# One order of accumulator banks for all four weight units of a transposed feed-forward chunk

## The chip, the cores and the metric

The kernel runs on one core of one Trainium2 chip. The metric is the device time of one execution in microseconds (us). Three runs are compared by their median, and one more execution was taken with a profile.

## What is computed

A two-layer decoder trunk over 256 tokens of width 1024, in float32. Each layer has four post-norm blocks: a SwiGLU feed-forward half-step, an attention mixer (forgetting attention in layer 0, latent attention in layer 1), a second feed-forward half-step, and a gated per-layer input embedding. The part that matters here is the half-step, which is run four times:

```python
D_MODEL, SEQ, DEPTH, D_FF = 1024, 256, 2, 2816
ALPHA = (2 * DEPTH) ** 0.25

def swiglu(x, w_in, w_out):
    h = x @ w_in
    gate, up = h[..., :D_FF], h[..., D_FF:]
    return (jax.nn.silu(gate) * up) @ w_out

def post_norm(x, delta, g, b):
    return layer_norm(ALPHA * x + delta, g, b)

for i in range(DEPTH):
    x = post_norm(x, 0.5 * swiglu(x, ffn1_w_in[i], ffn1_w_out[i]), ...)
    x = post_norm(x, mix(x), ...)
    x = post_norm(x, 0.5 * swiglu(x, ffn2_w_in[i], ffn2_w_out[i]), ...)
    x = post_norm(x, gate * (p[i] @ ple_w_proj[i]), ...)
```

## The kernel before

Every product of float32 matrices is made of three matmuls on split operands: both factors are written as a high part and a low remainder in a reduced format, and `mm3` adds high x high, high x low and low x high into one accumulator. ScalarE makes the high part of a weight unit (line 171) and VectorE the remainder (line 172). Such a split fills one of a handful of slots (`hl0` to `hl9`, and `qk`, `fs`, `ota`, `otb` when they are lent).

The order of the work is written out by hand. Weights come in groups over the DMA queue of SyncE into three raw buffers, and a planner (`Stream`) decides where in the instruction stream the next unit is split: `pump`, called at the end of each `mm3`, compares a running estimate of each engine's time with the arrival of the next group. That estimate grows by the number of columns of each matmul. `use` hands out a unit, and splits it first if it isn't split yet.

A feed-forward half-step (`ffn`) works through 11 chunks of 256 hidden columns, each with its gate and its up half. Chunks 0 and 1 are made token-major (`H`, in the first half-step partly by `first`): for each half of the tokens (`t`) the gate and the up half land side by side in one accumulator bank. Then `act` reads the bank, ScalarE with Silu over the gate half (line 630) and VectorE with a multiply by the up half (line 631). `T` transposes chunk 0 with four transposes.

Chunks 2 to 10 are unit-major and transposed (`HT`), in three groups: 2, 3, 4, then 5, 6, 7, then 8, 9, 10, with the output products (`W`) of finished chunks after each group, and four transposes ahead of the second group and of the third. An HT chunk takes two banks, `ps[0]` for the gate and `ps[1]` for the up half; the ring of banks is `h` for even chunks and `tr` for odd ones, with two banks each. `H` takes one bank of `h` at a time. Of its four weight units (`u`), each holds two slices of the contraction (`kk`), and each slice has four blocks of 128 hidden columns (`b`): blocks 0 and 1 go to `ps[0]`, blocks 2 and 3 to `ps[1]`. One block of one slice is one `mm3`, that is three weight loads and three matmuls of 256 columns, so a unit has 24 matmuls and a chunk 96. When all four units are through, ScalarE applies Silu to `ps[0]` (line 663), VectorE multiplies by `ps[1]` (line 664), and the product is split in two parts (lines 496 and 497) as the stationary operand of `W`.

A first write into a bank waits until the last reader of the tile that stood there is done; the wait stands at the first weight load of that write. All matmuls of `mm` have line 487, all transposes line 491.

Of the kernel before, what the change touches and what calls it, by code (L numbers as in the profile page):

```python
# [394 lines left out]
class Trunk:  # L395
# [180 lines left out]
    def ffn(self, li, which, lni, kv=False, ple=False, at=None, cold=False):  # L576
# [69 lines left out]
        def HT(c):  # L646
            ring = "h" if c % 2 == 0 else "tr"
            ps = [self.bank(ring) for _ in range(2)]
            for u in range(4):
                w = self.use(("win", li, which, c, u))  # L650
                steps = [(kk, b) for kk in range(2) for b in range(4)]
                if u == 0:
                    steps.sort(key=lambda s: s[1] // 2)
                for kk, b in steps:
                    k = 2 * u + kk
                    o = ps[b // 2][:, 256 * (b % 2) : 256 * (b % 2) + 256]
                    col = slice(512 * kk + 128 * b, 512 * kk + 128 * b + 128)
                    self.mm3(
                        o, lambda i: w[:, i, col], lambda i: self.xT[:, :, i, k, :],
                        k == 0 and b % 2 == 0, k == 7 and b % 2 == 1,  # L660
                    )
            gt = self.tl([128, 768], F32, "P", 2)[:, 0:512]
            nc.scalar.activation(gt, ps[0], AF.Silu)  # L663
            nc.vector.tensor_tensor(gt, gt, ps[1], op=ALU.mult)  # L664
            self.S.busy(act=512, dve=512)
            o = self.tl([128, 2, 512], F32R, "g4", 5)
            self.parts(o[:, 0, :], o[:, 1, :], gt)
            gT[c] = o
# [31 lines left out]
        for i, group in enumerate(GROUPS):  # L700
            if i == 1:
                T(1, "h")
            if i == 2:
                if kv:
                    self.kv_transpose()
                elif ple:
                    self.ple_transpose()
                else:
                    spare = self.bank("tr")
                    for k in range(4):  # L710
                        self.transpose(spare[:, 128 * k : 128 * k + 128], self.ident)
            for c in group:
                for f in at.get(c, ()):
                    f()
                if c == 4:
                    self.load_gb(li, lni)
                HT(c)
            if i == 1 and kv:
                self.flush()
                self.kv_transpose_rope()  # L720
            if i == 2 and ple:
                self.ple_project(li)
            while late and (late[0] <= group[-1]) and not (i == 0 and late[0] == 1):
                W(late.pop(0), both)
# [780 lines left out]
```

## Time and profile before

| | |
|---|---|
| three runs | 1097.37, 1095.62, 1091.08 us |
| median | 1095.62 us |
| profiled execution | 1097.88 us, span 1095.7 us |
| mean granted TensorE clock | 0.997 |
| TensorE matmuls busy | 1078.4 us, 7160 matmuls |
| VectorE busy | 711.9 us |
| ScalarE busy | 540.7 us |
| HBM read | 196.81 MB, 181 GB/s over the span with what is written |

Rows of the timeline and of the chain of waits begin with the start in microseconds from the begin of the span and the length in microseconds; then come the engine, the line, and the tiles written and read ("h<-xT,hl": bank of ring h, from the activations and a weight slot), and how many instructions are merged in the row. PE is TensorE's matmul, PEld its weight load, DVE VectorE, ACT ScalarE, POOL GpSimd and SP SyncE. Matmuls overlap in the pipeline, so the pace of a row is read from the distance of two starts. The view of one line ends with those who waited for it. A group row ends with the busy time in microseconds, the mean of one in nanoseconds, and the idle time before with its releaser.

### The profile page before, as it was taken

What the parts mean: (1) busy time and instruction counts of PE and PEld (TensorE: products, weight loads), DVE (VectorE), ACT (ScalarE), POOL (GpSimd) and SP (SyncE); (2) the same over time, 40 slices, a digit from 0 to 9 for tenths busy, and PEclk for the clock granted to TensorE, in tenths of its full rate; (3) what the DMA queues carried; (4) which work ended last, traced back from release to release, by engine and by line L of the source; (5) the groups of instructions that cost most, each with busy time, mean ns of one, the idle gap of its engine ahead of it and who ended that gap; (6) DMA issues with size and microseconds to landing.
All of it is one profiled execution on the core that took longest, in us unless ns stands there. A gap on an engine that the chain in (4) does not pass through costs nothing.

```text
span 1095.7 us, 17634 instructions
## 1 busy us (share of the span) xinstructions
PE 1078.4 (98%) x7160; PEld 978.4 (89%) x7160; DVE 711.9 (65%) x1010; ACT 540.7 (49%) x792; POOL 76.5 (7%) x128
## 2 busy tenths in 40 slices
PE   9999999999999999999999999999999999999997
PEld 6999999899879999998899999988999789898986
DVE  5665545788797545558966554388666885555566
ACT  5564433666646444444565443345655464444431
POOL 0000000222200000000320000011111000000000
PEclk9999999999999999999999999999999999999999
DMA  8886652444358856455578554344453668565502
GB/s 274 289 283 236 195 187 93 154 151 158 118 162 280 286 166 192 153 187 161 162 278 265 191 177 166 93 104 132 142 163 103 194 220 290 194 203 192 174 19 77
DMA packets 150676, 199.00 MB, mean 182 GB/s; under 512 B 11842, under 2 KB 128578, under 8 KB 150596
## 3 DMA queue, kind: packets, MB, share of 16 engines
q1 hardware_dynamic: 150596, 197.88, 55.7%
q8 instruction: 56, 0.92, 0.3%
q14 instruction: 24, 0.20, 0.1%
HBM read 196.81 MB, written 1.05 MB: 181 GB/s over the span
## 4 chain that ended last, share of the span: by engine, by line
PE 88%; DVE 7%; ACT 2%; issue 1%; POOL 1%; DMA 0%; DVEq 0%; SPq 0%; ACTq 0%; POOLq 0%
PE h L487 36%; PE y L487 30%; PE tr L487 19%; DVE hl L172 2%; PE tr L491 2%; DVE x L564 1%; DVE st L549 1%; DVE x L548 1%; ACT hl L171 1%; POOL rs L559 1%; PE y L465 1%; DMA raw<-in_ffn_w_in_dram 0%; DVE xT L497 0%; PE tr L1021 0%; DVE g L790 0%
## 5 line engine op out<-in xcount | busy, mean ns | idle before, releaser
L172 DVE TENSOR_TENSOR hl<-raw,hl 128x1024 fp32r<-128x1024 f32 (+3 forms) x287 | 333.6, 1183 | 159.7 <-ACT hl L171 158.5
L171 ACT ACTIVATE hl<-raw 128x1024 fp32r<-128x1024 f32 (+3 forms) x287 | 285.3, 1018 | 185.0 <-PE y L487 87.3
L487 PE MATMUL h<-xT,hl 128*128 128x256 f32 x2064 | 245.1, 279 | 0.9 <-DVE qk L497 0.9
L487 PEld LDWEIGHTS h<-xT,hl 128*128 128x128 f32 x2064 | 240.5, 188 | 2.1 <-DVE qk L497 1.1
L487 PE MATMUL y<-hl,g 128*128 128x512 f32 x780 | 181.0, 390 | 0.0
L487 PEld LDWEIGHTS y<-hl,g 128*128 128x128 f32 x780 | 145.7, 188 | 29.8
L487 PE MATMUL tr<-xT,hl 128*128 128x256 f32 x888 | 105.5, 278 | 0.0
L487 PEld LDWEIGHTS tr<-xT,hl 128*128 128x128 f32 x888 | 103.6, 188 | 0.1
L487 PE MATMUL h<-hl,xT 128*128 128x512 f32 (+1 forms) x396 | 94.5, 388 | 0.7 <-DVE xT L497 0.4
L487 PEld LDWEIGHTS h<-hl,xT 128*128 128x128 f32 x396 | 72.4, 188 | 17.1 <-DVE xT L497 1.1
L487 PE MATMUL y<-hl,xT 128*128 128x512 f32 (+2 forms) x312 | 60.8, 349 | 0.2 <-DVE xT L497 0.2
L487 PEld LDWEIGHTS y<-hl,xT 128*128 128x128 f32 x312 | 50.7, 188 | 7.5 <-DVE xT L497 0.7
L559 POOL TENSOR_TENSOR rs<-ve,mhalf 128x1 f32<-128x1 f32 x16 | 15.2, 950 | 525.0 <-DVE ve L558 525.0
L496 ACT ACTIVATE xT<-tr 128x512 fp32r<-128x512 f32 x34 | 19.2, 597 | 57.9 <-PE tr L491 57.9
L497 DVE TENSOR_TENSOR g<-P,g 128x512 fp32r<-128x512 f32 x36 | 24.9, 692 | 25.2 <-ACT g L496 25.2
L496 ACT ACTIVATE g<-P 128x512 fp32r<-128x512 f32 x36 | 22.8, 632 | 31.0 <-DVE P L664 31.0
L487 PE MATMUL y<-hl,ota 128*128 128x512 f32 x144 | 36.9, 400 | 0.0
L172 DVE TENSOR_TENSOR qk<-raw,qk 128x1024 fp32r<-128x1024 f32 x21 | 25.7, 1223 | 10.7 <-ACT qk L171 10.5
L172 DVE TENSOR_TENSOR otb<-raw,otb 128x1024 fp32r<-128x1024 f32 (+1 forms) x20 | 24.0, 1202 | 13.1 <-ACT otb L171 13.1
L663 ACT ACTIVATE P<-h 128x512 f32<-128x512 f32 x20 | 12.0, 598 | 41.5 <-PE h L487 41.5
L664 DVE TENSOR_TENSOR P<-P,h 128x512 f32<-128x512 f32 x20 | 13.7, 687 | 27.8 <-PE h L487 26.1
L487 PEld LDWEIGHTS y<-hl,ota 128*128 128x128 f32 x144 | 26.8, 193 | 5.2
(240 smaller groups left out, 1399.3 us busy)
## 6 DMA issues: line engine op xcount, KB each, us to landing
raw<-in_ffn_w_in_dram SPq DMA_DIRECT2D x172, 512.0 KB, 5.1
raw<-in_ffn_w_out_dram SPq DMA_DIRECT2D x44, 1024.0 KB, 5.2
raw<-in_fox_w_in_dram SPq DMA_DIRECT2D x12, 1024.0 KB, 5.3
raw<-in_ple_w_gate_dram SPq DMA_DIRECT2D x8, 1024.0 KB, 5.0
raw<-in_mla_w_o_dram SPq DMA_DIRECT2D x8, 1024.0 KB, 5.0
gb<-in_ln_g_dram SPq DMA_DIRECT2D x8, 512.0 KB, 7.0
gb<-in_ln_b_dram SPq DMA_DIRECT2D x8, 512.0 KB, 7.5
raw<-in_fox_w_o_dram SPq DMA_DIRECT2D x4, 1024.0 KB, 5.1
```

Source lines behind the costliest of these rows:

```text
L171: nc.scalar.activation(hi[:, c], src[:, c], AF.Copy)
L172: nc.vector.tensor_tensor(lo[:, c], src[:, c], hi[:, c].bitcast(F32), op=ALU.subtract)
L465: self.nc.tensor.matmul(hot[:, 0:384], self.mask[:, 0:128], self.mask, start=True, stop=True)
L487: self.nc.tensor.matmul(out, lhsT, rhs, start=start, stop=stop)
L491: self.nc.tensor.transpose(out, in_, self.ident)
L496: self.nc.scalar.activation(hi, src, AF.Copy)
L497: self.nc.vector.tensor_tensor(lo, src, hi.bitcast(F32), op=ALU.subtract)
L548: nc.vector.scalar_tensor_tensor(xs, xs, alpha, y, op0=ALU.mult, op1=ALU.add)
L549: nc.vector.bn_stats(st, xs)
L559: nc.gpsimd.tensor_tensor(rs, ve, self.mhalf, op=ALU.pow)
L663: nc.scalar.activation(gt, ps[0], AF.Silu)
L664: nc.vector.tensor_tensor(gt, gt, ps[1], op=ALU.mult)
```

## The change

In unit 0 of every HT chunk the eight steps (slice, block) stood sorted by bank: slice 0 blocks 0, 1, slice 1 blocks 0, 1, and then slice 0 blocks 2, 3, slice 1 blocks 2, 3. Now they stand as in the other three units: slice 0 blocks 0, 1, 2, 3 and then slice 1 blocks 0, 1, 2, 3. The set of matmuls, their operands and the start and stop flags of each bank stay as they are.

```diff
             for u in range(4):
                 w = self.use(("win", li, which, c, u))
-                steps = [(kk, b) for kk in range(2) for b in range(4)]
-                if u == 0:
-                    steps.sort(key=lambda s: s[1] // 2)
-                for kk, b in steps:
+                for kk, b in ((kk, b) for kk in range(2) for b in range(4)):
                     k = 2 * u + kk
                     o = ps[b // 2][:, 256 * (b % 2) : 256 * (b % 2) + 256]
                     col = slice(512 * kk + 128 * b, 512 * kk + 128 * b + 128)
```

## The prediction

> **What bounds the kernel now.** I read the page first: the busy shares, the granted clock and the chain that ended last.
>
> ```profile
> span 1095.7 us, 17634 instructions
> ...
> PE 1078.4 (98%) x7160; PEld 978.4 (89%) x7160; DVE 711.9 (65%) x1010; ACT 540.7 (49%) x792; POOL 76.5 (7%) x128
> ...
> PEclk9999999999999999999999999999999999999999
> ...
> PE 88%; DVE 7%; ACT 2%; issue 1%; POOL 1%; DMA 0%; DVEq 0%; SPq 0%; ACTq 0%; POOLq 0%
> ```
>
> TensorE is busy for 98% of the span at an undiminished clock, and 88% of the chain is its own work. Whatever holds a matmul of a transposed chunk (HT) back is therefore paid in full, and whatever doesn't costs nothing. The chain in order of time then gives the pace of the chunks. There are 36 HT chunks in twelve groups of three (three groups to a feed-forward half-step), and here is one row of 96 matmuls from each group.
>
> ```profile
> 32.59 11.31 PE h L487 x96
> ...
> 88.75 10.90 PE tr L487 x96
> ...
> 143.62 10.90 PE h L487 x96
> ...
> 336.56 11.31 PE h L487 x96
> ...
> 392.70 11.31 PE tr L487 x96
> ...
> 448.87 10.90 PE h L487 x96
> ...
> 560.39 10.90 PE h L487 x96
> ...
> 615.26 10.90 PE tr L487 x96
> ...
> 670.38 11.31 PE h L487 x96
> ...
> 897.15 11.31 PE h L487 x96
> ...
> 953.32 10.90 PE tr L487 x96
> ...
> 1008.19 10.90 PE h L487 x96
> ```
>
> The reader is to see that the same instructions run at two paces: 11.31 / 96 = 117.8 ns a matmul in five groups, 10.90 / 96 = 113.5 ns in seven. Nothing in the code separates the five from the seven: the middle group is slow in one half-step and fast in three, with the same instructions around it. A slow chunk costs 0.41 us more, a slow group about 1.23 us. All five together, 6.2 us, are nearly the spread of the three runs shown (1091.08 to 1097.37), so I take the pace for something that each execution draws anew. The profiled execution took 1097.88 us, 2.26 above the median of 1095.62; two slow groups more than the median run would account for that.
>
> Third, the timeline of single units asks whether the order inside a unit has a price of its own. Each chunk has four weight units of 24 matmuls; unit 0 alone has the sorted order today.
>
> ```profile
> 43.73 2.99 PE L487 MATMUL tr<-xT,qk 128*128 128x256 f32 x24
> 46.56 2.99 PE L487 MATMUL tr<-xT,fs 128*128 128x256 f32 x24
> 49.39 5.82 PE L487 MATMUL tr<-xT,hl 128*128 128x256 f32 x48
> ...
> 110.37 5.60 PE L487 MATMUL tr<-xT,hl 128*128 128x256 f32 x48
> 115.81 2.88 PE L487 MATMUL tr<-xT,ota 128*128 128x256 f32 x24
> 118.53 2.88 PE L487 MATMUL tr<-xT,otb 128*128 128x256 f32 x24
> ```
>
> Read the distances between starts. In the slow chunk unit 0 (sorted, slot qk) takes 46.56 - 43.73 = 2.83 us and unit 1 (alternating, slot fs) takes 49.39 - 46.56 = 2.83 us. In the fast chunk units 0 and 1 together take 115.81 - 110.37 = 5.44, that is 2 x 2.72, and unit 2 takes 118.53 - 115.81 = 2.72. Sorted and alternating cost the same to 0.01 us in either pace.
>
> **The change, part by part.** *Order of matmuls.* In unit 0 of each of the 36 chunks two triples of block columns 2 and 3 (second bank, first contraction slice) change places with two of columns 0 and 1 (first bank, second slice): 12 matmuls with their 12 weight loads are moved, none added or taken away. By the unit rows the price is 36 x 0.00 = 0; bounded by the 0.01 us that those rows resolve, at most 36 x 0.01 = 0.36 us either way.
>
> *What is not moved.* The planner is called after each triple and counts only columns, which are equal, so each split of a weight unit and each DMA that it triggers is issued behind the same number of triples; SP's and POOL's queues are passed by nothing. The unit is split as a whole before its first matmul, and both slices of the activations were already used by the chunks before, so no operand is wanted before it is there. Unit 3 is unchanged, so the activation and the multiply behind the chunk start as they did.
>
> *The wait that comes forward.* The first write to the second bank stands at matmul 13 today and at matmul 7 afterwards. It has to wait until the bank's last reader is through. From the second chunk of each group on, and in the groups that begin with chunks 5 and 8, that reader is the multiply of line 664 of the same ring's previous chunk, or a set of transposes, at least a whole chunk earlier (10.9 us or more); its cover stays huge. Only chunk 2, the first of each half-step, follows at once on an H chunk that used the same bank: its reader is the multiply of line 631. The view of that line:
>
> ```profile
> L631 DVE TENSOR_TENSOR g<-g,h x8: 406/420/422, 27.1 to 897.2; 128x256 f32<-128x256 f32 x8
> ...
> who waited for it (us, times):
> busy tenths in 40 slices 0000000000000000000000000000000000000000
> ```
>
> Nobody waits for it today. The four places where chunk 2 begins, each as the first seven weight loads and the multiply that they run against:
>
> ```profile
> 32.32 0.89 PEld L487 LDWEIGHTS h<-xT,hl 128*128 128x128 f32 x7
> ...
> 32.60 0.42 DVE L631 TENSOR_TENSOR g<-g,h 128x256 f32<-128x256 f32 x1 [1.05 <-ACT g L630]
> ...
> 336.29 0.89 PEld L487 LDWEIGHTS h<-xT,hl 128*128 128x128 f32 x7
> ...
> 336.57 0.42 DVE L631 TENSOR_TENSOR g<-g,h 128x256 f32<-128x256 f32 x1 [1.26 <-ACT g L630]
> ...
> 560.12 0.89 PEld L487 LDWEIGHTS h<-xT,hl 128*128 128x128 f32 x7
> ...
> 560.41 0.42 DVE L631 TENSOR_TENSOR g<-g,h 128x256 f32<-128x256 f32 x1 [1.05 <-ACT g L630]
> ...
> 896.88 0.89 PEld L487 LDWEIGHTS h<-xT,hl 128*128 128x128 f32 x7
> ...
> 897.17 0.42 DVE L631 TENSOR_TENSOR g<-g,h 128x256 f32<-128x256 f32 x1 [0.67 <-ACT g L630]
> ```
>
> A load of this group takes 0.19 us (the row of its group is the first of the next fence), so in the first place the seventh begins at 32.32 + 0.89 - 0.19 = 33.02; the multiply ends at 32.60 + 0.42 = 33.02. In the others it is 336.99 against 336.99, 560.82 against 560.83, 897.58 against 897.59. The seventh load would start just as its release comes, so what counts is how long a release travels from VectorE to a weight load:
>
> ```profile
> L487 PEld LDWEIGHTS h<-xT,hl 128*128 128x128 f32 x2064 | 240.5, 188 | 2.1 <-DVE qk L497 1.1
> ...
> 225.00 0.42 DVE L497 TENSOR_TENSOR qk<-h,qk 128x256 fp32r<-128x256 f32 x1
> ...
> 225.48 0.30 PEld L487 LDWEIGHTS h<-xT,hl 128*128 128x128 f32 x2 [1.08 <-DVE qk L497]
> ```
>
> 225.48 - 225.42 = 0.06 us. So each of the four is held for about 0.06 us: 4 x 0.06 = 0.24 us. Queued behind the held load on TensorE are all the rest of chunk 2, and through it everything later; other engines have slack. Today the release has six matmuls more, 6 x 0.118 = 0.70 us, of cover. The price lies between 0 (a load that hides inside the matmul before it) and 4 x 0.70 = 2.8 us, all of the cover used up, where the multiply is late; I take 0.24, since all four places lie within 0.01 us of the same alignment.
>
> *The pace.* A held load lets the matmul stream of chunk 2's group start again, and the rows show that a group keeps the pace with which it started. So four groups draw again: three that were slow here (32, 336, 896) and one that was fast (560). Bounds: all four fast, 3 x 1.23 = 3.7 us won; all four slow, 1.23 lost, on this execution. No row shows a hold this short in the middle of such a group, so I take the shares of the twelve rows, five slow to seven fast, before as after, which adds nothing to a median.
>
> *A rule that speaks against it.* By the page's clock row the granted clock stands at nine tenths or more in all 40 slices, though units 1 to 3 go through both banks twice each. The Trainium skill, "TensorE: Matmul & The Clock Gate", section "A second HAM failure mode: psum-queue depth-cycling", warns that cycling through the banks makes small idles that throttle the clock; if it held here, unit 0 would run slow too, while the trace's alternating units disagree with it.
>
> **Sum.** On the profiled execution with its paces kept, 1097.88 + 0.24 = 1098.1 us; on the median run 1095.62 + 0.24 = 1095.9 us, which is my forecast: no change that can be told. About 0.5% (5.5 us) is what a measurement of this kernel tells from no change; its three runs lie 6.3 us apart.
>
> **The rivals.**
> 1. *The multiply is late, and the wait is a real one: slower.* VectorE also carries the splits in order; one of 1.2 us ahead of line 631 would end the multiply that much later. The bracket of 0.67 to 1.26 us idle before the four multiplies speaks against it; only an idle that falls to nothing would begin to cost. From then on each place costs what the multiply is late, at most 0.70 us: 1095.62 + 2.8 = 1098.4. Chance 0.12.
> 2. *The held load leaves its group at the fast pace: faster.* For it: seven of twelve groups are fast. Against: three of the four chunk 2 groups started slow. On the profiled execution 1097.88 + 0.24 - 3.7 = 1094.4. Chance 0.12.
> 3. *It leaves its group at the slow pace: slower.* 1097.88 + 0.24 + 1.23 = 1099.4; from a run in which all four are fast it would be 4 x 1.23 + 0.24 = 5.2 us. Chance 0.09.
> 4. *Alternation halves the clock in unit 0.* 36 units of 2.72 us would take twice that, 98 us more: 1194. The equal units 0 and 1 above speak against it. Chance 0.01. This is what the skill's rule on bank cycling would come to.
>
> **How the numbers follow.** The forecast keeps 0.66. Within it the draw of the paces may put one median beyond 0.5%, 0.08 on either side (0.053 each). Of rival 1 I give a quarter to slower than that (0.03), of rival 2 three tenths to faster (0.036), of rival 3 four tenths to slower (0.036), and rival 4 wholly (0.01): faster 0.09, slower 0.13, the same 0.78. The range: at the low end the profiled execution without its five slow groups, 1097.88 - 6.2 + 0.24 = 1091.9, and the fastest run shown, 1091.08, so 1091.0; at the high end the profiled execution with rival 1's full price, 1097.88 + 2.8 = 1100.7. Rival 4 and the tails are left out.
>
> **What would show it.** Right: a waits view with a few hundredths of a microsecond of weight loads for line 631, four times, at the seventh load of chunk 2; unit 0 as long as unit 1 in every chunk; groups in only the two paces, with their number of slow ones telling the total to about 1.2 us each. Rival 1 would show line 631 among the releasers with several tenths, and VectorE busy up to the multiply. Rivals 2 and 3 would show all four chunk 2 groups at one pace, in more than one run. Wrong altogether: a change in the pace of groups that begin with chunk 5 or 8 in all runs alike, a third pace, unit 0 longer or shorter than unit 1, or other counts of splits and DMAs between the matmuls.

## The result and the profile after

| | kernel before | changed kernel |
|---|---|---|
| median of 20 runs, us | 1095.72 | 1096.30 |
| lowest to highest, us | 1091.08 to 1099.90 | 1093.70 to 1099.73 |
| profiled execution, us (span) | 1097.88 (1095.7) | 1096.81 (1094.7) |

The ratio after to before is 1.0003, with a 95% interval of 0.9992 to 1.0015: no change that can be told. The page of the changed kernel has the same instructions and shares:

```profile
span 1094.7 us, 17634 instructions
...
PE 1077.1 (98%) x7160; PEld 976.9 (89%) x7160; DVE 713.1 (65%) x1010; ACT 541.1 (49%) x792; POOL 76.5 (7%) x128
...
PEclk9999999999999999999999999999999999999999
...
PE 87%; DVE 7%; ACT 2%; issue 1%; DMA 1%; POOL 1%; SPq 0%; DVEq 0%; ACTq 0%; POOLq 0%
```

The chain in order of time, with the row of the first chunk of each of the twelve groups (start, length, engine, tile and line, matmuls):

```profile
32.08 11.36 PE h L487 x96
...
88.25 10.90 PE tr L487 x96
...
143.12 10.90 PE h L487 x96
...
335.96 10.98 PE h L487 x96
...
390.92 10.90 PE tr L487 x96
...
445.79 10.90 PE h L487 x96
...
557.30 11.36 PE h L487 x96
...
613.52 10.90 PE tr L487 x96
...
668.63 11.31 PE h L487 x96
...
897.32 10.98 PE h L487 x96
...
952.28 10.90 PE tr L487 x96
...
1007.15 10.90 PE h L487 x96
```

Two things are to be seen. The first chunk of a group took 11.31 or 10.90 us before; the four that are chunk 2 now take 11.36, 10.98, 11.36 and 10.98, that is 0.05, 0.08, 0.05 and 0.08 more, 0.26 us in all. These are the four holds, and no other chunk has one. And the pattern of paces is another: three groups at 118 ns a matmul (32, 557, 668) where the profile before had five.

The first of the holds, by the multiply that releases the bank and the seventh weight load of chunk 2:

```profile
32.09 0.42 DVE L631 TENSOR_TENSOR g<-g,h 128x256 f32<-128x256 f32 x1 [0.52 <-ACT g L630]
...
32.57 0.19 PEld L487 LDWEIGHTS h<-xT,hl 128*128 128x128 f32 x1
```

The multiply ends at 32.51 and the load starts 0.06 us behind it. At the pace of the loads ahead of it, it would have started at about 32.50.

The timeline of single units, in the same chunk as before (the third of the second group; units 0 and 1 are merged in the first row, and their distances were 5.44 and 2.72 us):

```profile
109.87 5.60 PE L487 MATMUL tr<-xT,hl 128*128 128x256 f32 x48
115.31 2.88 PE L487 MATMUL tr<-xT,ota 128*128 128x256 f32 x24
118.03 2.88 PE L487 MATMUL tr<-xT,otb 128*128 128x256 f32 x24
```

115.31 - 109.87 = 5.44 and 118.03 - 115.31 = 2.72: unit 0 costs the same in the new order.

Three groups in place of five should have saved 2.5 us, the holds cost 0.26, yet the two profiles differ by 1.07. The windows of the latent attention show where most of the rest is. Columns: stretch, length, matmul busy time (matmuls), granted clock, share and rate of the DMA engines. Before:

```profile
756.00:760.00 4.00, 4.00 (x35) 1.00 0.00 0
760.00:764.00 4.00, 2.09 (x16) 1.00 0.57 150
764.00:768.00 4.00, 4.00 (x23) 0.64 0.45 121
768.00:772.00 4.00, 4.00 (x26) 0.94 0.39 159
```

After:

```profile
756.00:760.00 4.00, 3.55 (x29) 1.00 0.11 26
760.00:764.00 4.00, 2.53 (x13) 0.78 0.51 138
764.00:768.00 4.00, 4.00 (x15) 0.50 0.84 266
768.00:772.00 4.00, 4.00 (x24) 0.87 0.00 0
```

TensorE idles there for 4.00 - 2.09 = 1.9 us before, and for 0.45 + 1.47 = 1.9 us after, at the start of the first product with the attention weights. Two rows of the timeline before, with the idle time ahead in brackets:

```profile
762.98 0.39 PE L487 MATMUL h<-PT,g 128*128 128x256 f32 x1 [1.70 <-ACT PT L496]
763.57 0.79 PE L487 MATMUL h<-PT,g 128*128 128x256 f32 x5 [0.21 <-DVE PT L497]
```

Behind that the clock is halved, for (0.36 + 0.06) x 4 / 0.5 = 3.4 us before and for (0.22 + 0.50 + 0.13) x 4 / 0.5 = 6.8 us after. A stretch of 3.4 us at half clock does 1.7 us less work, so the changed kernel's profile should be about 2.5 - 0.26 - 1.7 = 0.5 us shorter; the other half microsecond of the 1.07 is not accounted for. The Trainium skill, "TensorE: Matmul & The Clock Gate", section "What's actually happening", gives the window of that gate as 3413 ns and the lower clock as half; the trace agrees with both (one and two stretches of 3.4 us, 0.50 in the row that lies within). The Trainium skill's section "Why this matters for your kernels" on the same page warns of idle gaps over about 3 us; here idle times of 1.7 and 0.2 us were enough, and the measurement decides. They are not enough each time: the same two waits stand in eleven of the fourteen profiles of this document, and two half-clock stretches follow in two of them, one in six and none in three.

### The profile page after: what moved, and what is told of

It reads as the page before. It is cut to its first block, busy times and chain, and to the rows that moved or that the text cites. A ratio compares the mean times of both kernels' runs of the same rounds, so it can differ in the third digit from the quotient of the medians.

```text
span 1094.7 us, 17634 instructions
## 1 busy us (share of the span) xinstructions
PE 1077.1 (98%) x7160; PEld 976.9 (89%) x7160; DVE 713.1 (65%) x1010; ACT 541.1 (49%) x792; POOL 76.5 (7%) x128
## 4 chain that ended last, share of the span: by engine, by line
PE 87%; DVE 7%; ACT 2%; issue 1%; DMA 1%; POOL 1%; SPq 0%; DVEq 0%; ACTq 0%; POOLq 0%
PE h L487 36%; PE y L487 30%; PE tr L487 19%; DVE hl L172 2%; PE tr L491 2%; DVE x L564 1%; DMA raw<-in_ffn_w_in_dram 1%; DVE st L549 1%; DVE x L548 1%; ACT hl L171 1%; POOL rs L559 1%; DVE xT L497 0%; PE tr L1018 0%; DVE g L787 0%; DVE g L497 0%
```

## The experiments

All of them change the order in chunk 2, what stands ahead of the groups, or the idle time of the latent attention. "Pace" is the distance of starts in the middle of a group: 113.3 or 117.8 ns, never another.

**The new order in chunk 2 alone, and everywhere but there.**

Against the kernel before:

```diff
                 steps = [(kk, b) for kk in range(2) for b in range(4)]
-                if u == 0:
+                if u == 0 and c != 2:
                     steps.sort(key=lambda s: s[1] // 2)
```

> The alternating order in chunk 2 of each half-step alone, the other 32 chunks sorted as before. Theory (the wait on the multiply of line 631 is the whole cost): four intervals of some 0.175 to 0.18 us between the sixth and the seventh matmul of chunk 2 in place of 0.113 to 0.118, that is about 0.06 us each and 0.25 us in all, and no other interval changed; after each hold the group may go on at either pace (113 or 118 ns). Rival (alternation itself costs): no hold worth naming, and units 0 of chunks 3 to 10 shorter than in the changed kernel. Total between 1091 and 1100 us by either, told by the paces.

The counterpart has `c == 2` in place of `c != 2`:

> The sorted order kept in chunk 2 alone, the alternating one in the 32 other chunks. Theory (only chunk 2 carries a cost): no hold anywhere, units 0 of 2.82 to 2.91 us at the head of a group and 2.72 or 2.83 elsewhere, as in the kernel before. Rival (alternation has a price of its own): units 0 of chunks 3 to 10 longer than units 1.

With the new order in chunk 2 alone the interval behind the seventh matmul (the expectation named the one ahead of it, but the recorded start of the seventh matmul stays where it was, and that of the eighth moves) is 179, 175, 179 and 180 ns, and the four first chunks are these:

```profile
32.17 11.36 PE h L487 x96
...
337.34 11.36 PE h L487 x96
...
559.97 11.36 PE h L487 x96
...
899.77 11.36 PE h L487 x96
```

All four went on at 118 ns, though all four had begun at 113. With chunk 2 sorted there is no hold: the four take 11.31, 10.90, 10.90 and 11.31 us, and the chunks behind them 11.31 or 10.88. So the alternating order makes a hold in chunk 2 only, about 0.065 us in each place. The two kernels took 1100.49 and 1094.48 us. The holds are the least part of these 6 us: the first had six groups at 118 ns and two half-clock stretches, the second four and none, and 2 x 1.28 + 2 x 1.7 + 0.26 = 6.2 (a group at the slower pace costs 288 x 4.45 ns = 1.28 us). The two slow groups more are groups of chunk 2, four against two. Whether the holds made them slow, so that they belong to the price of the order, one execution of each kernel cannot tell.

**The second bank earlier still.** Chunk 2 with the second bank at the second triple, and the new order in the 32 other chunks:

```diff
-                if u == 0:
-                    steps.sort(key=lambda s: s[1] // 2)
+                if u == 0 and c == 2:
+                    steps = [(0, 0), (0, 2), (0, 1), (0, 3)] + steps[4:]
```

> In unit 0 of chunk 2 the second bank comes with the second triple, at matmul 4. Theory: cover shorter by three matmuls than in the changed kernel, so a hold of 0.06 + 3 x 0.115 = 0.41 us between the third and the fourth matmul, four times, 1.6 us in all. Rival (a fixed price for a wait that is not met at once): about 0.06 us as in the changed kernel. Whether the group goes on fast after a hold that is longer than the 0.28 us of one matmul: fast in all four if an empty pipeline decides it, mixed if the moment does.

The view of line 631 now names who waits, and the weight load's row has the idle time ahead of it:

```profile
L631 DVE TENSOR_TENSOR g<-g,h x8: 408/418/422, 26.6 to 896.7; 128x256 f32<-128x256 f32 x8
...
who waited for it (us, times):
  PEld h L487: 1.6, 4
  PE h L487: 0.4, 1
```

The third interval is 417, 641, 417 and 415 ns in place of 113 to 118, and the next 222 to 226, since the pipeline fills anew (the first interval of every group is 200 to 208 ns): 0.30 + 0.11 = 0.41 us in three places, as the cover of three matmuls would have it, and 0.65 in the one at 336 us. There VectorE was late:

```profile
335.28 1.22 DVE L172 TENSOR_TENSOR fs<-raw,fs 128x1024 fp32r<-128x1024 f32 x1
336.42 0.41 DVE L631 TENSOR_TENSOR g<-g,h 128x256 f32<-128x256 f32 x1
336.83 0.69 DVE L497 TENSOR_TENSOR g<-tr,g 128x512 fp32r<-128x512 f32 x1
```

A split of 1.22 us runs right up to the multiply, which so ends about 0.23 us later than it would have. After the holds two groups went on at 118 and two at 113 ns, so that a longer hold decides nothing about the pace.

**The second bank first.**

Again with the new order in the other chunks:

```diff
-                if u == 0:
-                    steps.sort(key=lambda s: s[1] // 2)
+                if u == 0 and c == 2:
+                    steps.sort(key=lambda s: 1 - s[1] // 2)
```

> In unit 0 of chunk 2 the second bank's twelve matmuls come first, so that it is wanted at matmul 1. Theory (the cover is 0.118 us for each matmul ahead of the second bank): the first weight load waits until about 0.054 us after the multiply of line 631, some 0.76 us in each of four places, 3.0 us in all over the kernel before (ratio about 1.0025 to 1.003). After so long a wait the pipeline is empty; groups that started from an empty pipeline in the forgetting attention all went fast (113 ns), so the four groups of chunk 2 should be fast. Rival (a wait there hides behind something else): under 1 us in all, and paces as before.

This expectation failed: 1095.94 us against 1095.92, ratio 0.9998 (0.9980 to 1.0016), and no hold in the trace.

```profile
31.86 0.89 PEld L487 LDWEIGHTS h<-xT,hl 128*128 128x128 f32 x7
31.89 0.94 PE L487 MATMUL h<-xT,hl 128*128 128x256 f32 x6
32.15 0.42 DVE L631 TENSOR_TENSOR g<-g,h 128x256 f32<-128x256 f32 x1 [1.06 <-ACT g L630]
```

The first load starts at 31.86, before the multiply has begun. So the bank written first isn't the one that the multiply still reads. It seems that the tile that is written first gets the ring's older bank, whichever name it has, and the multiply's bank goes to the one written second; no view names the banks. In chunk 2 this kernel is then the sorted order with the names of two banks exchanged, and again has the cover of twelve matmuls. What counts is the place of the second bank, not which half of the chunk it holds. The groups of chunk 2 began at 113, 113, 118 and 118 ns.

**Both kernels once more.**

> The changed kernel once more. If the pace is drawn anew in each execution, the twelve groups show another pattern of 113 and 118 ns than in its first profile (there slow at 32, 557 and 668 us only), while the four holds stand again at 0.06 us. If the pattern belongs to the kernel, it is the same again. The total follows the number of slow groups at 1.2 to 1.3 us each and the number of half-clock windows in the latent attention.

> The kernel before once more. No hold in chunk 2 (intervals six to seven 113 or 118 ns). If the pace is drawn in each execution, the groups of chunk 2 show another pattern than slow, slow, fast, slow. By the profiles so far the four groups that begin with chunk 8 should repeat theirs: fast, fast, slow, fast. If holds make slow groups, the chunk 2 groups without a hold here should be slow in well under 10 of 16 places.

The changed kernel took 1094.76 us with four groups at 118 ns (32, 557, 668 and 948) and no half-clock stretch; its holds were 0.05 to 0.07 us each. The kernel before took 1098.94 with six (chunk 2 at 32, 336 and 897, others at 392, 670 and 953) and one stretch. Each kernel repeats its own first profile in eleven groups of twelve, those of chunk 2 in all four (slow, fast, slow, fast with the change, and slow, slow, fast, slow before); in both, the one that differs is chunk 5 of the last half-step. So the expectation of another pattern in chunk 2 failed: in these profiles the pattern belongs to the kernel more than to the execution. It cannot belong to the kernel alone, since the runs of the kernel before beside these lie between 1091.13 and 1101.73 us, which is several slow groups. Chunk 8 repeats itself in every half-step, as expected. Six profiles have the cover of twelve matmuls in chunk 2 and four transposes ahead: the kernel before twice, chunk 2 sorted, the second bank first, and two kernels below (transposes in order, idle time filled). In these its groups were at 118 ns 14 times in 23 where nothing held them; after a hold 10 times in 16. These shares agree, but they are small counts, and the way there differs. Of the twelve groups held at the seventh load (the changed kernel twice, and the new order in chunk 2 alone) eleven had begun at 113 ns; the hold turned eight of these to 118 and the twelfth from 118 to 113.

**What sets the pace: the order of the transposes ahead?** On the kernel before:

```diff
-            for t in range(2):
-                for kt in range(2):
+            for kt in range(2):
+                for t in range(2):
```

> On the kernel before: the four transposes ahead of a group write their bank's quarters in order 0, 1, 2, 3 everywhere, in place of 0, 2, 1, 3 in T and in the transposition of the shared keys. In six profiles the groups behind transposes in order (chunk 8 in three half-steps) were fast 18 times of 18, the one behind 0, 2, 1, 3 for the shared keys slow 6 of 6, and those behind T mixed. Theory A (the order of these four writes sets the pace): all twelve groups fast in nearly every execution, three to five slow groups less at 1.25 us each, a ratio of 0.995 to 0.997. Theory B (something else ahead of the group, its timing or its operands, sets it): chunk 8 of the third half-step stays slow, and the ratio is 0.999 to 1.001.

The transposition of the shared keys is changed in the same way. 1096.55 us against 1096.64, ratio 0.9995 (0.9978 to 1.0011), with four groups at 118 ns, chunk 8 of the third half-step among them. Theory A fell.

**Or their number?** On the kernel before, the second kernel with `range(1)`:

```diff
+            if c in (2, 5) or (c == 8 and kv):
+                for k in range(4):
+                    nc.tensor.transpose(ps[0][:, 128 * k : 128 * k + 128], self.ident, self.ident)
```

> On the kernel before: four transposes of the identity (result overwritten) ahead of the nine groups that are not always fast, as the kernel has them already ahead of chunk 8 of the first half-step, whose group was fast in all profiles so far. Theory A (these transposes set the pace of what follows): no slow group, 4 to 5 x 1.25 us saved for 9 x 0.44 = 3.9 us added, the time near 1089.5 + 3.9 + 1.7 for each half-clock stretch, that is 1093.4 to 1096.8. Theory B (they do not): three to six slow groups as before, 1097 to 1103.

> The same with one transpose of the identity in place of four (9 x 0.11 = 1.0 us). Theory A: no slow group, 1090.5 to 1094. If it takes all four, or theory B: three to six slow groups, 1094 to 1101. In all of them the time should be 1089.5 + what is added + 1.25 for each slow group + 1.7 for each half-clock stretch, to about 0.5 us, as it was in the ten profiles before.

Neither theory was right. With eight transposes ahead in place of four, all eight groups of chunks 2 and 5 ran at 118 ns, and chunk 8 of the third half-step, at 118 in each of ten profiles so far, ran at 113: 1104.23 us. First chunks of the third half-step:

```profile
563.99 11.31 PE h L487 x96
...
620.56 11.31 PE tr L487 x96
...
677.38 10.90 PE h L487 x96
```

With five ahead, seven of the eight groups of chunks 2 and 5 ran at 113 ns, and chunk 8 again at 118: 1095.11 us.

```profile
556.75 10.90 PE h L487 x96
...
611.73 10.90 PE tr L487 x96
...
666.95 11.31 PE h L487 x96
```

So the number of matmuls ahead turns the paces, in opposite ways for these places, as far as one execution of each kernel goes.

**The idle time in the latent attention filled.** On the kernel before, ahead of the first product of the attention weights with the values:

```diff
+            if h == 0:
+                for _ in range(12):
+                    nc.tensor.matmul(ps[:, 0:256], self.xT[:, 0, 0, 0, :], self.xT[:, :, 0, 0, :], start=True, stop=True)
```

> On the kernel before: twelve matmuls more (128x256, their result is overwritten by the bank's first real one) ahead of the first attention product of the latent attention, where TensorE waits 1.7 us and where the profiles show none, one or two stretches of 3.4 us at half clock behind. Theory: the added 1.4 us lie within the wait, the clock does not fall, and one stretch or two of about 1.7 us are saved, ratio 0.997 to 0.999, with the granted clock at 1.00 in that stretch of the profile. Rival (the fall comes from the idle time around it, or the fill delays what it waits for): the half clock stays, ratio 1.000 to 1.001.

```profile
756.00:760.00 4.00, 4.00 (x36) 1.00 0.00 0
760.00:764.00 4.00, 3.51 (x27) 1.00 0.59 159
764.00:768.00 4.00, 4.00 (x28) 1.00 0.43 126
768.00:772.00 4.00, 4.00 (x35) 1.00 0.36 145
```

The clock stays whole where it was halved, and the wait is 0.29 us in place of 1.70. By itself this profile shows little, as three of the eleven without these matmuls lost no clock either; but the two kernels below that have them lost none as well, so it is three of three. The time, 1095.31 us against 1096.64, ratio 0.9992 (0.9974 to 1.0010), doesn't tell the gain from none by itself. In this execution one multiply of line 631 at 336 us was so late, again behind a split of 1.22 us, that even the sorted order was held there, by 0.6 us.

**All of it together.** One transpose more ahead of chunks 2 and 5, four ahead of chunk 8 of the third half-step, and the filled idle time; once on the changed kernel, once on the kernel before.

```diff
+            for k in range(1 if c in (2, 5) else 4 if c == 8 and kv else 0):
+                nc.tensor.transpose(ps[0][:, 128 * k : 128 * k + 128], self.ident, self.ident)
```

> The changed kernel (alternating order everywhere) with one more transpose ahead of chunks 2 and 5, four ahead of chunk 8 of the third half-step, and the twelve matmuls in the wait of the latent attention. Theory: (1) the transpose pushes the seventh load of chunk 2 back by 0.11 us, more than the 0.06 us by which its release is late, so the four holds go; (2) the number of transposes ahead sets the pace, so that none to two groups are slow; (3) no half-clock stretch. 1089.5 + 8 x 0.11 + 0.44 + 0 to 2 x 1.25 = 1090.8 to 1093.3, against about 1096 before: ratio 0.9955 to 0.9975. Rival (the pace of single profiles was chance): four to five slow groups, 1096 to 1097, ratio 0.999 to 1.001.

> The same additions on the kernel before (unit 0 sorted). Theory: as there is no hold in either, the same time and paces as its twin with the alternating order within what the measurement can tell, 1090.8 to 1093.3. If the alternating order has a price apart from the hold, this one is faster than its twin by more than the two intervals' width.

On the changed kernel 1092.77 us, ratio to the kernel before 0.9984 (0.9969 to 0.9999); on the kernel before 1092.26 us, ratio 0.9973 (0.9962 to 0.9983). Both times lie where they were expected and both are a little faster than the kernel before, though the first one's ratio is nearer to 1 than was forecast, since the kernel before had a median of 1094.77 us beside them. The medians of the two lie 0.5 us apart, with the sorted order ahead, and their intervals overlap: the times show no price of the alternating order apart from the hold, but do not exclude one of about 1 us. The changed kernel was not run beside them. Each has one group at 118 ns and no half-clock stretch. The first chunks on the changed kernel:

```profile
32.40 10.90 PE h L487 x96
...
335.44 10.90 PE h L487 x96
...
556.94 10.90 PE h L487 x96
...
891.80 11.31 PE h L487 x96
```

None has the 0.05 to 0.08 us of the hold: the one transpose of 0.11 us hides it.

## Why the prediction was right

**The sum held.** 4 x 0.06 = 0.24 us stood for the wait; the chain has 0.26. It was right for the reason given: the seventh load comes as its release leaves VectorE and waits for the way of the release. The load at 32.57, 0.06 us behind the end of the multiply, is this wait. The 0.41 us for three matmuls less, and no hold where twelve matmuls lie ahead of the second bank and the multiply is in time, show the cover of 0.113 to 0.118 us a matmul. The reader that it named, line 631, is the one. The sign of 0.6 us between the medians fits the sum, but at an interval of 0.9992 to 1.0015 it shows nothing.

**The order itself costs nothing**, as read from the unit rows: 36 x 0.00 stands, by the changed kernel's units and by the kernel that has the new order everywhere but in chunk 2.

**The pace.** That the paces of the four groups would add nothing to a median was assumed from seven groups to five. The medians agree with it, and so do the shares of slow groups (14 of 23 without a hold, 10 of 16 with one). Neither shows equal odds: one slow group more in every execution would be 1.28 us, and the interval of the ratio reaches from 0.9 us faster to 1.6 slower. How it came about was not foreseen. A group does not always keep the pace with which it began: the holds at the seventh load turned eight of eleven groups from 113 to 118 ns. That these groups had begun at 113 more often (11 of 12) than those without a hold (9 of 23), and so ended at much the same share, is luck as far as these runs show. And "something that each execution draws anew" was too simple: two profiles of one kernel agree in eleven groups of twelve, chunk 8 came out alike in its half-step in all ten profiles that have the four transposes ahead, and the number of transposes turns the paces of the rest.

**The spread of the runs** was put down to the paces alone, 6.2 us of 6.3. That step was incomplete. Fitted to the fourteen profiled executions the time is 1089.5 us, plus 1.28 for each group at 118 ns, plus 1.7 for each half-clock stretch of the latent attention, plus the holds and what was added; what remains lies between 0.8 below and 0.6 above. The clock row, nine tenths or more in all slices of 27 us, hid a stretch of 3.4 us, and "at an undiminished clock" was not quite true.

**The rivals.** Rival 1, the late multiply, happens: 0.23 us late in one of four places with the second bank at the second triple, and late enough to hold even the sorted order once, in the kernel with the filled idle time. These are two of the 56 places in fourteen profiles, both in the second half-step, and none of them is in the changed kernel. It was right to price it, and right that it isn't the rule. Rivals 2 and 3, one pace for all four groups, did not come in the two profiles of the changed kernel, which have two groups of four at each pace; with the new order in chunk 2 alone all four were at 118 ns, in one execution. What rival 3 says of a single hold came eight times in eleven, and the times do not rule out that it costs the changed kernel something, up to the 1.6 us at the end of the interval. Rival 4, a clock that falls by alternating banks, is out: 5.44 us for units 0 and 1 as before. The Trainium skill's section on psum-queue depth-cycling ("TensorE: Matmul & The Clock Gate") doesn't apply to these back-to-back matmuls; the half clock came where TensorE waited, not where it changed banks.

**What to look for.** The prediction wanted the holds in the view of waits. A hold of 0.06 us isn't listed there (nobody waits for line 631 in the changed kernel's view); it shows in the lengths of chunks, while the longer ones, of 0.34 us and more in the row of the load, are listed. One of its signs of being wrong altogether is there in part: the group of chunk 5 in the second half-step was at 118 ns in both profiles of the kernel before and at 113 in both of the changed kernel. The order isn't needed for that, as the two kernels that have the sorted order everywhere and only other transposes or the filled idle time had it at 113 too.

**Open.** Why the pace is 113 or 118 ns, and how the number of transposes turns it, is not settled; that kernels which differ in this number alone (eight or five ahead) have other paces is shown, with one execution of each; the mechanism is not. Nor is it known why groups of chunk 2 began at 113 ns more often with the new order. That chunk 8 of the other half-steps always runs at 113 ns fell with the last kernel, where one in 42 did not.

## What to carry to other kernels

The order of accumulator banks mattered here only where the bank that is written second has a late reader: count the matmuls ahead of its first write against that reader's end plus the way of the release, and look there alone. Which name came second was of no account here, only which bank was written second. Before reading a difference of some tenths of a percent, take apart what the executions differ in anyway (here the pace of groups and a half-clock stretch), since it can be ten times the effect.

## What the hardware did that I had not expected

The same stream of weight loads and 256-column matmuls holds one of two paces, 113.3 or 117.8 ns, for all 288 matmuls of a group, and a hold of 0.06 us or one more transpose of 0.11 us ahead can turn it: with five transposes ahead of chunks 2 and 5 it was 113 in 22 groups of 24, with eight in none of eight, in one execution. And a wait of 1.7 us followed by one of 0.2 us was enough in eight profiles of eleven to lose half the clock for 3.4 or 6.8 us; with twelve matmuls without use in that wait it stayed whole in three of three.
